# Feed-forward of three fused blocks: first pairs, sums of x, and the turn from up to down

## The chip, the core and the metric

The kernel runs on one core of one Trainium2 chip. The metric is the device time of one execution in microseconds (us), as the median of the runs shown. PE is the matmul engine (PEld its weight load), DVE the vector engine, ACT the scalar engine, POOL the GpSimd engine, and SP the engine that here only issues DMAs.

## What is computed

Three blocks run one behind another on x of 1024 tokens by 1024 features, all in float32. Blocks 1 and 2 end in a feed-forward of the same shape, and the change touches those two alone:

```
hn = norm(h)                                   # 1024 x 1024
g, up = jnp.split(hn @ w_ffn_in, 2, axis=-1)   # w_ffn_in 1024 x 5632
h = h + (jax.nn.silu(g) * up) @ w_ffn_out      # w_ffn_out 2816 x 1024
```

Block 1 has a root-mean-square norm ahead of it; block 2 has a layer norm and, between norm and feed-forward, a gated projection (the `ple` loop, L1207 to L1216). The up pass is the product with `w_ffn_in` and silu times up; the down pass is the product with `w_ffn_out` and the sum into h. "The turn" below is where one follows the other.

## The kernel before

**Two halves of every number.** A float32 operand x is kept as a high part `hi` (x rounded to fp32r) and a low part `lo` = x − hi. A product is three matmuls, hi·hi, hi·lo and lo·hi, added up in PSUM (`mm3`, L95 to L97); each is 128x128 by 128x512. So each operand that is loaded needs a cast (hi) and a subtraction (lo). For weights this is `weight` (L78 to L88): a DMA on SP's queue into one of two `w_raw` buffers, the cast on DVE (or on ACT where `hi_on` is set), the subtraction on POOL, into one of four pairs of buffers `w_hi`, `w_lo` of the pool `wp`.

**The up pass** (`ffn_up`) works on 22 pairs, each one column block of the gate weights and one of the up weights, with 128 features of the hidden layer. x lies in two halves of tokens, `x_fm[0]` (tokens 0 to 511) and `x_fm[1]` (512 to 1023).

- The first two pairs (`plain=2`) are plain products: 24 matmuls for each of g and u in each half of the tokens, 192 matmuls in all.
- The other 20 pairs use a scheme of seven products in place of eight (Strassen-Winograd), with x and the weights cut into quarters. A product is 12 matmuls, a pair 84. On the x side the products take, in their order, `b11`, `t1`, `t2`, `b21`, `t3`, `b12`, `b22`. The `b` are the quarters of x themselves, `t1` to `t3` sums of them, which `sums()` makes while the plain pairs run. `last_sums()` overwrites `b12`, which is a quarter of `x_fm[1]`, so it can only run when the plain pairs need `x_fm[1]` no more; its result is wanted by product 5 (counted from 0). Per k in 0 to 3 the sums are 4 subtractions or adds of 128x512 on POOL in `sums()` and 2 in `last_sums()`, and 5 and 2 on DVE.
- On the weight side `operands(fi)` makes seven operands for a pair: two loads of raw weights, four sums (one on POOL, three on DVE), seven casts on ACT, seven subtractions on POOL. An operand takes half of a `w_hi`, `w_lo` pair. These places come round in fives: four pairs in `wp`, and a fifth pair in the up pass's own pool. Six operands are made ahead (`more(AHEAD)`), then one behind each product (`more(1)`).
- The result of a pair, `ao`, is stored to `act_d` in HBM by SP, one half at a time.

**The down pass** takes the 22 row blocks of `w_ffn_out` in nine groups of two and a last group of four. `load` brings one block of activations back from `act_d` (SP's queue), ACT makes hi (L550), DVE makes lo (L551). A group is 16 sums of 128x512 in PSUM, each 12 matmuls for four blocks or 6 for two, and for each sum DVE adds into h (L562). The activations for the next group are asked for one group ahead. In block 1 the buffers for them come from twelve (`unit`, which held x and the sums), in block 2 from four (`unit_b`); each load takes whichever buffer comes free.

**The residual h** is written to HBM ahead of the up pass, since its place (32 KB of each partition) is used by the up pass: `t2` lies over h[4] to h[7], and the buffers `s` and the fifth pair `w_hi`, `w_lo` lie over h[0] to h[3]. It is read back at the turn by eight DMAs on ACT's queue (L570).

**Order.** The program's text sets priorities; a planner runs the text against a model of the engines and fixes each engine's order, so that a matmul that is ready in the model can pass one that is not. On the chip each engine then runs its list in order and waits by semaphores. SP's and ACT's DMA issues stand in such lists too.

Of the kernel before, what the change touches and what calls it, by code (L numbers as in the profile page):

```python
# [13 lines left out]
ALU = mybir.AluOpType  # L14
# [17 lines left out]
def kernel(ctx: ExitStack, tc: tile.TileContext, a, out, blocks=(1, 2, 3)):  # L32
# [15 lines left out]
    def f(ap):  # L48
        return ap.bitcast(F32)
# [80 lines left out]
    def fm(w, xh, nk=KD, k0=0, pt=None, start=True, stop=True):  # L130
        pt = mmtile() if pt is None else pt
        mm3(pt, [(kslice(w, k0 + k), xslice(xh, k, 0, HS)) for k in range(nk)], start, stop)
        return pt
# [243 lines left out]
    def ffn_up(pl, pp, unit, unit_r, x_fm, w_in, act_d, plain=2):  # L377

        half_k = lambda h, k: tuple(fm_.at[4 * k][0] for fm_ in x_fm[h])
        b11, b21, b12, b22 = half_k(0, 0), half_k(0, 1), half_k(1, 0), half_k(1, 1)
        t1, t3 = (tuple(four(unit(f"{n}{j}")) for j in range(2)) for n in ("t1", "t3"))
        t2 = tuple(four(unit_r(f"t2{j}")) for j in range(2))
        dve, pool_e = nc.vector.tensor_tensor, nc.gpsimd.tensor_tensor
        sl = [slice(0, HS), slice(HS, S)]
        tmp = lambda n: pl.tile([P, HS], F32, name=n, tag=n, bufs=2)

        def whole(n, x, k, eng):
            o = tmp(n)  # L390
            eng(out=o, in0=f(x[0][:, k]), in1=f(x[1][:, k]), op=ALU.add)
            return o

        def parts(x, k, src, eng):
            act(out=x[0][:, k], in_=src, func=AF.Copy)
            eng(out=x[1][:, k], in0=src, in1=f(x[0][:, k]), op=ALU.subtract)

        def sums():

            for k in range(4):  # L400
                x11, x12, x22 = whole("p1", b11, k, pool_e), whole("u2", b12, k, dve), whole("u3", b22, k, pool_e)
                dve(out=x11, in0=x12, in1=x11, op=ALU.subtract)
                parts(t1, k, x11, pool_e)
                yield
                dve(out=x12, in0=x22, in1=x12, op=ALU.subtract)
                parts(t3, k, x12, pool_e)
                dve(out=x22, in0=x22, in1=x11, op=ALU.subtract)
                parts(t2, k, x22, dve)
                yield

        def last_sums():

            for k in range(4):
                x21, y2 = whole("p1", b21, k, pool_e), whole("u2", t2, k, dve)
                dve(out=x21, in0=x21, in1=y2, op=ALU.subtract)
                parts(b12, k, x21, pool_e)

        def out_of(fi):
            ao = pl.tile([P, S], F32, name="ao", tag="ao", bufs=2)
            return ao, lambda h: nc.sync.dma_start(act_d[fi][:, sl[h]], ao[:, sl[h]])  # L420

        gen = sums()
        for fi in range(plain):
            wg, wu = weight(w_in[fi]), weight(w_in[F_TILES + fi])
            ao, store = out_of(fi)
            for h in (1, 0):
                g = fm(wg, x_fm[h])
                u = fm(wu, x_fm[h])
                silu_mul(pl, g, u, ao, sl[h])
                store(h)  # L430
                for _ in range(2 if fi < plain - 1 or h else 8):
                    next(gen, None)


        n_op, held = [0], []

        def slot():
            if n_op[0] % 2 == 0:
                i = n_op[0] // 2 % 5
                q, nb = (wp, 4) if i < 4 else (pl, 1)  # L440
                held[:] = [q.tile([P, 1024], F32R, name=n, tag=n, bufs=nb) for n in ("w_hi", "w_lo")]
            c = slice(n_op[0] % 2 * 512, n_op[0] % 2 * 512 + 512)
            n_op[0] += 1
            return tuple(x[:, c] for x in held)

        def operand(src, eng):
            hi, lo = slot()
            nc.scalar.copy(hi, src)  # L448
            eng(out=lo, in0=src, in1=f(hi), op=ALU.subtract)  # L449
            return hi, lo  # L450

        def operands(fi):
            raw = []
            for j in (F_TILES + fi, fi):
                r = wp.tile([P, 1024], F32, name="w_raw", tag="w_raw", bufs=2)
                nc.sync.dma_start(r, w_in[j])
                raw.append(r)
            (a21, a22), (a11, a12) = ((r[:, 0:512], r[:, 512:1024]) for r in raw)

            def mix(x, y, op, eng):  # L460
                s = pl.tile([P, 512], F32, name="s", tag="s", bufs=4)
                eng(out=s, in0=x, in1=y, op=op)
                return s
            yield operand(a11, pool_e)
            s1 = mix(a21, a22, ALU.add, pool_e)
            yield operand(s1, pool_e)
            s2 = mix(s1, a11, ALU.subtract, dve)
            yield operand(s2, pool_e)
            s4 = mix(a12, s2, ALU.subtract, dve)
            s3 = mix(a11, a21, ALU.subtract, dve)  # L470
            yield operand(a12, pool_e)
            yield operand(s3, pool_e)
            yield operand(a22, pool_e)
            yield operand(s4, pool_e)

        AHEAD = 6
        xs = (b11, t1, t2, b21, t3, b12, b22)
        ready = []

        def all_operands():  # L480
            for fi in range(plain, F_TILES):
                yield from operands(fi)
        source = all_operands()

        def more(n):
            for _ in range(n):
                w = next(source, None)
                if w is not None:
                    ready.append(w)
        more(AHEAD)  # L490
        last_sums()
        for fi in range(plain, F_TILES):
            ao, store = out_of(fi)

            def product(i, pt, start=True):
                w = ready.pop(0)
                mm3(pt, [(kslice(w, k), tuple(x[:, k] for x in xs[i])) for k in range(4)], start, onto=not start)
            pa, pd = mmtile("mm", 2), mmtile("mm", 2)
            pb, pc = (pp.tile([P, HS], F32, name=n, tag=n, bufs=1) for n in ("pb", "pc"))
            p1, u2, u3 = tmp("p1"), tmp("u2"), tmp("u3")  # L500
            product(0, pa)
            act(out=p1, in_=pa, func=AF.Copy)
            more(1)
            product(1, pc)
            more(1)
            product(2, pb)
            tt(out=u2, in0=p1, in1=pb, op=ALU.add)
            more(1)
            product(3, pa, False)
            sg = tmp("sg")  # L510
            act(out=sg, in_=pa, func=AF.Silu)
            more(1)
            product(4, pb, False)
            tt(out=u3, in0=p1, in1=pb, op=ALU.add)  # L514
            tt(out=p1, in0=u3, in1=pc, op=ALU.add)
            more(1)
            product(5, pd)
            tt(out=u3, in0=u3, in1=pd, op=ALU.add)
            tt(out=ao[:, sl[0]], in0=sg, in1=u3, op=ALU.mult)
            store(0)  # L520
            more(1)
            product(6, pc, False)
            tt(out=u2, in0=u2, in1=pc, op=ALU.add)
            act(out=u2, in_=u2, func=AF.Silu)
            tt(out=ao[:, sl[1]], in0=u2, in1=p1, op=ALU.mult)
            store(1)
            more(1)

    def ffn(x_fm, unit, unit_b, h, h_d, h_st, open_h, w_in, w_out, before_last, done, group=2):
# [9 lines left out]
        with ExitStack() as c:  # L539
            pool("down_edge", side="right", c=c).tile([P, 24], F32, name="edge")  # L540
            dp = pool("down", side="right", c=c)

            def load(fi, last):
                if last:
                    hi, lo = (dp.tile([P, S], F32R, name=f"act_{j}", tag=f"act_{j}", bufs=LAST) for j in ("hi", "lo"))
                else:
                    at = unit_b("act")
                    hi, lo = at[:, 0:S], at[:, S:2 * S]
                nc.sync.dma_start(f(lo), act_d[fi])
                act(out=hi, in_=f(lo), func=AF.Copy)  # L550
                nc.vector.tensor_tensor(out=lo, in0=f(lo), in1=f(hi), op=ALU.subtract)  # L551
                return hi, lo

            def down(fis, ats, done=None):
# [11 lines left out]
            groups = [list(range(g, g + group)) for g in range(0, F_TILES - LAST, group)]  # L566
            groups.append(list(range(F_TILES - LAST, F_TILES)))
            ats = [[load(fi, False) for fi in groups[0]]]
            for t in range(NT):
                nc.scalar.dma_start(h[t], h_d[t * P:(t + 1) * P])  # L570
            for i, fis in enumerate(groups[:-1]):
                nxt_g = groups[i + 1]
                ats.append([load(fi, nxt_g is groups[-1]) for fi in nxt_g])
                down(fis, ats[i])
            before_last()
            down(groups[-1], ats[-1], done)
            done.flush()
# [1056 lines left out]
```

## Time and profile before

| | |
|---|---|
| median of the 3 runs | 3503.18 us (3501.65 to 3503.7) |
| the profiled execution | 3509.02 us, its span 3507.3 us |
| mean granted clock of PE | 0.962 |
| feed-forward of block 1 in the span | about 716 to 1480 us, its turn at 1166 to 1201 us |
| feed-forward of block 2 in the span | about 2106 to 2820 us, its turn at 2546 to 2580 us |

The span runs from the first to the last instruction; the 1.7 us around it are start and end. The views give busy time by engine, the idle time ahead of an instruction and what ended it ("idle before", in brackets in a timeline), and the clock that PE was granted in a stretch.

### The profile page before, as it was taken

Reading aid. Unit: us, or ns where it says so; the run is one execution under the profiler, and the core shown is the slowest. Engines: PE = TensorE matmul, PEld = TensorE weight load, DVE = VectorE, ACT = ScalarE, POOL = GpSimd, SP = SyncE. Lnnn points to the kernel's source line nnn. Section 1 sums busy time; section 2 is a strip of 40 time slices with the busy share of each in tenths; the row PEclk is TensorE's granted clock in tenths of the full one; section 3 lists DMA queues with packets and bytes.
Section 4 is the critical chain, followed back from the end, with each engine's and each line's share of the span. In section 5 each row is a group of like instructions: output and inputs, shape, how many; then the busy total and the mean of one; then the engine's idle time right before and its main releaser. Section 6 shows DMA issues by size and latency. Waiting matters only on the chain. (4 is left out here: it accounts for less than half of the span.)

```text
span 3507.3 us, 40024 instructions
## 1 busy us (share of the span) xinstructions
PE 3278.3 (93%) x14976; PEld 2674.0 (76%) x14976; DVE 2169.9 (62%) x3300; ACT 1066.3 (30%) x2002; POOL 1368.6 (39%) x906
## 2 busy tenths in 40 slices
PE   8999999989999899999979998999989986889998
PEld 6888888877888678778768776888867865667776
DVE  5455456374444666557768847444467779985665
ACT  3333311132233200312145522323210133445552
POOL 3111131175555222134444348555412356552221
PEclk9999999999999999999989999999999998999899
DMA  4111124322222521222251132222342221122241
GB/s 138 65 62 62 55 66 132 127 66 78 82 83 83 216 73 58 75 88 94 87 180 49 37 108 75 81 81 88 105 148 96 85 75 38 49 91 73 77 144 66
DMA packets 111986, 310.12 MB, mean 88 GB/s; under 512 B 15744, under 2 KB 20992, under 8 KB 111792
## 3 DMA queue, kind: packets, MB, share of 16 engines
q1 hardware_dynamic: 79184, 240.75, 20.4%
q10 hardware_dynamic: 32560, 66.69, 5.6%
q8 instruction: 118, 1.93, 0.2%
q14 instruction: 76, 0.62, 0.1%
q0 software_dynamic: 48, 0.13, 0.0%
HBM read 235.62 MB, written 72.15 MB: 88 GB/s over the span
## 5 line engine op out<-in xcount | busy, mean ns | idle before, releaser
L87 POOL TENSOR_TENSOR w_lo<-w_raw,w_hi 128x1024 fp32r<-128x1024 f32 x187 | 467.1, 2499 | 1224.7 <-DVE w_hi L86 888.3
L95 PE MATMUL mm<-x,w_hi 128*128 128x512 f32 x688 | 278.4, 405 | 22.7 <-DVE kl L279 11.0
L96 PE MATMUL mm<-x,w_hi 128*128 128x512 f32 x688 | 277.7, 404 | 0.0
L97 PE MATMUL mm<-x,w_lo 128*128 128x512 f32 x688 | 274.9, 400 | 0.5 <-POOL w_lo L87 0.5
L86 DVE CAST w_hi<-w_raw 128x1024 fp32r<-128x1024 f32 x179 | 188.7, 1054 | 126.2 <-PE mm L96 57.3
L449 POOL TENSOR_TENSOR w_lo<-s,w_hi 128x512 fp32r<-128x512 f32 x160 | 220.4, 1385 | 113.6 <-ACT w_hi L448 112.1
L95 PE MATMUL mf<-x,w_hi 128*128 128x512 f32 x576 | 233.8, 406 | 16.4 <-DVE u L1299 14.2
L97 PE MATMUL mf<-x,w_lo 128*128 128x512 f32 x576 | 229.5, 398 | 1.2 <-POOL w_lo L87 1.2
L96 PE MATMUL mf<-x,w_hi 128*128 128x512 f32 x576 | 230.2, 400 | 0.0
L449 POOL TENSOR_TENSOR w_lo<-w_raw,w_hi 128x512 fp32r<-128x512 f32 x120 | 166.7, 1389 | 106.8 <-ACT w_hi L448 106.8
L562 DVE TENSOR_TENSOR h<-h,mm 128x512 f32<-128x512 f32 x214 | 145.0, 683 | 96.8 <-PE mm L97 88.6
L514 DVE TENSOR_TENSOR u<-p,pb 128x512 f32<-128x512 f32 x40 | 27.5, 687 | 267.1 <-PE pb L97 267.1
L95 PE MATMUL mm<-w_hi,act 128*128 128x512 f32 x384 | 153.6, 400 | 25.4 <-DVE h L562 24.9
L95 PEld LDWEIGHTS mm<-x,w_hi 128*128 128x128 f32 x688 | 132.2, 192 | 55.4 <-issue 24.0
L448 ACT CAST w_hi<-s 128x512 fp32r<-128x512 f32 x160 | 97.3, 619 | 236.5 <-PE pc L96 152.2
L1313 DVE SCALAR_TENSOR_TENSOR cy<-u,cols,cy 128x1024 f32<-128x1024 f32 x80 | 166.3, 2084 | 0.9
L97 PEld LDWEIGHTS mm<-x,w_lo 128*128 128x128 f32 x688 | 131.8, 192 | 28.9 <-issue 1.5
L96 PEld LDWEIGHTS mm<-x,w_hi 128*128 128x128 f32 x688 | 132.3, 192 | 27.0 <-issue 2.0
L96 PE MATMUL mm<-w_lo,act 128*128 128x512 f32 x384 | 151.4, 394 | 0.0
L97 PE MATMUL mm<-w_hi,act 128*128 128x512 f32 x384 | 151.2, 394 | 0.0
L335 ACT ACTIVATE st<-st,nmax 128x128 f32<-128x128 f32 (+5 forms) x192 | 119.3, 623 | 104.0 <-DVE nmax L329 99.5
L95 PEld LDWEIGHTS mf<-x,w_hi 128*128 128x128 f32 x576 | 110.9, 192 | 41.1 <-DVE u L1299 14.9
(506 smaller groups left out, 8971.0 us busy)
## 6 DMA issues: line engine op xcount, KB each, us to landing
w_raw<-in_w_ffn_in_dram SPq DMA_DIRECT2D x88, 512.0 KB, 3.7
w_raw<-in_w_in_dram SPq DMA_DIRECT2D x78, 512.0 KB, 3.5
act_d<-ao SPq DMA_DIRECT2D x88, 256.0 KB, 2.0
w_raw<-in_w_ffn_out_dram SPq DMA_DIRECT2D x44, 512.0 KB, 3.5
act<-act_d SPq DMA_DIRECT2D x36, 512.0 KB, 3.4
w_raw<-in_w_out_dram SPq DMA_DIRECT2D x24, 512.0 KB, 3.8
gates_d<-go SPq DMA_DIRECT2D x32, 256.0 KB, 2.0
gt<-gates_d ACTq DMA_DIRECT2D x32, 256.0 KB, 3.1
```

Of the source, the lines that this page charges most:

```text
L86: nc.vector.tensor_copy(hi, raw)
L87: nc.gpsimd.tensor_tensor(out=lo, in0=raw, in1=f(hi), op=ALU.subtract)
L95: mm(out_, lh, rh, start=start and i == 0, stop=False, **kw)
L96: mm(out_, lh, rl, start=False, stop=False, **kw)
L97: mm(out_, ll, rh, start=False, stop=stop and i == n - 1, **kw)
L335: act(out=st[:, :w + extra], in_=st[:, :w + extra], func=AF.Exp, scale=-1.0, bias=nmax, accum_out=ssum)
L448: nc.scalar.copy(hi, src)
L449: eng(out=lo, in0=src, in1=f(hi), op=ALU.subtract)
L514: tt(out=u3, in0=p1, in1=pb, op=ALU.add)
L562: tt(out=hh, in0=hh, in1=pt, op=ALU.add)
L1313: stt(out=y, in0=src, scalar=w, in1=y, op0=ALU.mult, op1=ALU.add)
```

## The change

It edits `ffn_up` and `ffn`, which both feed-forwards use.

- The first of the two plain pairs takes the halves of the tokens in the order 0, 1 instead of 1, 0; the second stays at 1, 0.
- `more(AHEAD)` stands ahead of the second plain pair instead of behind both.
- `last_sums()` becomes a generator; its four steps are taken one behind each of the first four products, where all four stood ahead of the first product.
- The pair of places for operands that lies in the up pass's own pool is used for the first of five instead of the last of five.
- All buffers of the up pass's pool are named at its start, which fixes their order in memory.
- Activations of the down pass go round in six fixed buffers, in both blocks (block 1: six of `unit`; block 2: four of `unit_b`, two of `unit`).
- The subtraction that makes an activation's lo moves from DVE to POOL (all 22 blocks of a down pass).
- The casts of `w_ffn_out` move from DVE to ACT for the nine groups ahead of the last one (`hi_on`).
- The eight loads of h move from ACT's queue to SP's.

```diff
+        for n, w, dt, nb in ([("ao", S, F32, 2)] + [(n, HS, F32, 2) for n in ("sg", "p1", "u2", "u3")] +
+                             [("s", HS, F32, 4), ("w_hi", 1024, F32R, 1), ("w_lo", 1024, F32R, 1)]):
+            pl.tile([P, w], dt, name=n, tag=n, bufs=nb)
...
                 parts(b12, k, x21, pool_e)
+                yield
...
-        gen = sums()
-        for fi in range(plain):
-            wg, wu = weight(w_in[fi]), weight(w_in[F_TILES + fi])
-            ao, store = out_of(fi)
-            for h in (1, 0):
-                g = fm(wg, x_fm[h])
-                u = fm(wu, x_fm[h])
-                silu_mul(pl, g, u, ao, sl[h])
-                store(h)
-                for _ in range(2 if fi < plain - 1 or h else 8):
-                    next(gen, None)
...
-                q, nb = (wp, 4) if i < 4 else (pl, 1)
+                q, nb = (wp, 4) if i else (pl, 1)
...
-        more(AHEAD)
-        last_sums()
+        gen = sums()
+        for fi in range(plain):
+            wg, wu = weight(w_in[fi]), weight(w_in[F_TILES + fi])
+            ao, store = out_of(fi)
+            last = fi == plain - 1
+            if last:
+                more(AHEAD)
+            for h in (1, 0) if last else (0, 1):
+                g = fm(wg, x_fm[h])
+                u = fm(wu, x_fm[h])
+                silu_mul(pl, g, u, ao, sl[h])
+                store(h)
+                for _ in range(2 if not last or h else 8):
+                    next(gen, None)
+
+        fours = last_sums()
...
                 mm3(pt, [(kslice(w, k), tuple(x[:, k] for x in xs[i])) for k in range(4)], start, onto=not start)
+                next(fours, None)
...
+            acts = []
+
             def load(fi, last):
...
-                    at = unit_b("act")
+                    if len(acts) < 6:
+                        acts.append((unit_b if len(acts) < 4 else unit)("act"))
+                    at = acts[fi % 6]
...
-                nc.vector.tensor_tensor(out=lo, in0=f(lo), in1=f(hi), op=ALU.subtract)
+                nc.gpsimd.tensor_tensor(out=lo, in0=f(lo), in1=f(hi), op=ALU.subtract)
...
             ats = [[load(fi, False) for fi in groups[0]]]
+            hi_on[0] = True
             for t in range(NT):
-                nc.scalar.dma_start(h[t], h_d[t * P:(t + 1) * P])
+                nc.sync.dma_start(h[t], h_d[t * P:(t + 1) * P])
...
+            hi_on[0] = False
             before_last()
```

## Rows read from the trace of the kernel before

**Rows 1.** The page: busy time of each engine, share of the span, instructions.

```profile
PE 3278.3 (93%) x14976; PEld 2674.0 (76%) x14976; DVE 2169.9 (62%) x3300; ACT 1066.3 (30%) x2002; POOL 1368.6 (39%) x906
```

**Rows 2.** Windows: length, busy time (instructions) by engine, granted clock, DMA share, GB/s.

```profile
715.60:812.20 96.60, 81.98 (x335) 65.49 (x334) 69.08 (x64) 29.32 (x51) 74.40 (x47) 0.89 0.20 62
900.00:1000.00 100.00, 100.00 (x443) 82.81 (x442) 45.64 (x54) 30.17 (x53) 54.69 (x42) 1.00 0.26 86
...
1165.80:1201.00 35.20, 20.30 (x65) 14.91 (x65) 25.98 (x26) 12.82 (x13) 4.21 (x2) 0.76 0.83 321
1220.00:1300.00 80.00, 78.58 (x341) 63.27 (x341) 54.76 (x69) 4.25 (x4) 14.42 (x6) 1.00 0.19 66
...
2139.80:2193.60 53.80, 42.36 (x158) 32.27 (x158) 37.45 (x34) 15.72 (x28) 45.03 (x31) 0.84 0.18 59
...
2546.00:2580.00 34.00, 23.80 (x86) 18.39 (x85) 18.43 (x23) 4.64 (x5) 5.07 (x2) 0.85 0.64 232
2600.00:2700.00 100.00, 97.31 (x420) 77.76 (x419) 72.38 (x86) 8.50 (x8) 19.24 (x8) 1.00 0.25 85
2700.00:2780.00 80.00, 78.65 (x342) 63.41 (x341) 55.33 (x68) 4.25 (x4) 19.21 (x8) 1.00 0.30 99
```

**Rows 3.** Timeline of PE at the first up pass's start: start, us, operation.

```profile
705.17 1.04 PE L158 MATMUL tr<-sq_c,xn 128*128 128x128 f32 x8
...
720.68 1.94 PE L158 MATMUL tr<-sq_c,xn 128*128 128x128 f32 x8 [2.74 <-DVE rstd L148]
...
733.33 0.63 PE L95 MATMUL mm<-h,w_hi 128*128 128x512 f32 x1
```

**Rows 4.** Windows of POOL alone, both starts: length, busy time (instructions), then as above.

```profile
726.10:781.40 55.30, 50.35 (x33) 0.90 0.10 34
2118.10:2181.10 63.00, 60.30 (x39) 0.87 0.16 50
```

**Rows 5.** Waits of PE at the second start: us in total, times, longest.

```profile
PE mm L96 <- POOL y L396: 7.0, 2, 4.1
```

**Rows 6.** Timeline of PE at both turns.

```profile
1154.96 0.39 PE L97 MATMUL pb<-t,w_lo 128*128 128x512 f32 x1
...
1172.43 0.79 PE L95 MATMUL pc<-h,w_hi 128*128 128x512 f32 x1 [3.48 <-DVE p L515]
...
1177.29 0.62 PE L97 MATMUL pc<-h,w_lo 128*128 128x512 f32 x1
...
1190.54 0.79 PE L95 MATMUL mm<-w_hi,act 128*128 128x512 f32 x1 [11.26 <-DVE h L562]
...
2560.16 0.79 PE L95 MATMUL mm<-w_hi,act 128*128 128x512 f32 x1 [5.14 <-DVE h L562]
...
2569.06 0.79 PE L95 MATMUL mm<-w_hi,act 128*128 128x512 f32 x1 [4.31 <-DVE h L562]
```

**Rows 7.** Timeline of ACT and its queue at the first turn.

```profile
1183.10 1.06 ACT L550 ACTIVATE act<-act 128x1024 fp32r<-128x1024 f32 x1 [0.61 <-DMA act<-act_d]
1183.12 9.22 ACTq L570 DMA_DIRECT2D h<-h_d  x8
```

**Rows 8.** Reads of activations, 1140 to 1201 us: issue ns min/median/max, first and last start.

```profile
L549 SPq DMA_DIRECT2D act<-act_d x12: 319/380/433, 1149.7 to 1177.9; - x12
```

**Rows 9.** Timeline of DVE at the first turn.

```profile
1168.72 3.06 DVE L551 TENSOR_TENSOR act<-act 128x1024 fp32r<-128x1024 f32 x1
```

**Rows 10.** A window at the first turn, columns as in Rows 2.

```profile
1183.00:1192.40 9.40, 1.86 (x4) 1.49 (x5) 3.25 (x4) 1.07 (x2) 0.00 (x0) 0.59 1.03 418
```

**Rows 11.** Groups of DVE, 2580 to 2780 us: count, busy us, mean ns, idle before.

```profile
L562 DVE TENSOR_TENSOR h<-h,mm 128x512 f32<-128x512 f32 x91 | 61.5, 683 | 39.2 <-PE mm L97 39.2
...
L86 DVE CAST w_hi<-w_raw 128x1024 fp32r<-128x1024 f32 x18 | 28.7, 1592 | 0.4
L551 DVE TENSOR_TENSOR act<-act 128x1024 fp32r<-128x1024 f32 x14 | 26.0, 1856 | 0.0
```

**Rows 12.** Groups of POOL, 2580 to 2780 us, columns as in Rows 11.

```profile
L87 POOL TENSOR_TENSOR w_lo<-w_raw,w_hi 128x1024 fp32r<-128x1024 f32 x18 | 43.3, 2403 | 180.3 <-DVE w_hi L86 174.2 <-PE mm L97 4.1 <-PE mf L97 1.4
```

## Prediction

> **What bounds the kernel now.** I read the page's busy times first: PE is busy 93% of the span and no other engine over 62% [rows 1], so PE's list of matmuls sets the end, and a change gains only where PE stands still or runs at its lower clock. Then windows over the two feed-forwards, to price that in one measure: in a stretch without waits PE ends 443 instructions in 100 us, 0.2257 us each [rows 2]; what a window is longer than its count times 0.2257 is lost, idle time and slow clock together. Five places lose, and the diff edits work at all of them.
>
> - Start 1 (715.6 to 812.2): 335 instructions, of them 32 transposes that take 1.04 us per eight where nothing holds them up [rows 3]. 303 × 0.2257 + 4.2 = 72.6 of 96.6: 24.0 lost.
> - Start 2 (2139.8 to 2193.6): 158 × 0.2257 = 35.7 of 53.8: 18.1 lost.
> - Turn 1: 65 × 0.2257 = 14.7 of 35.2: 20.5 lost. Turn 2: 86 × 0.2257 = 19.4 of 34.0: 14.6 lost.
> - Down passes, three windows: 341, 420 and 342 instructions in 80, 100 and 80 us: 3.0 + 5.2 + 2.8 = 11.0 lost [rows 2].
>
> Together 88 us, the most that the change can give. Next I read, in the timelines of PE and of what released it, what ends each wait.
>
> **Start 1: order of the halves.** PE ends the projection into h at 715.6 and then has only the transposes of the last token tiles, with waits between them, one of 2.74 us, on DVE, since each tile wants a norm first [rows 3]. The first matmuls of the up pass are in the second half of the tokens, which those transposes fill. The waits also cost clock: behind them a matmul stands at 0.63 us (733.33), the lower of the clock's two levels (1.2 and 2.4 GHz), where 0.39 is usual, and the granted clock over the whole start is 0.89 [rows 2, 3, 6]. With half 0 first, 48 matmuls (10.8 us) need nothing of those tiles; with the transposes' 4.2 they fill 715.6 to 730.6, just when the second half is whole. PE alone could then win all 24 us.
>
> POOL does not let it. It is busy 50.35 of the 55.3 us up to 781.4, when the last subtraction of `last_sums` is done, in 33 instructions, 1.53 us each [rows 4]. By count these are 16 for `sums`, 8 for `last_sums`, 2 adds and 6 subtractions for operands, and one weight. The sums need the second half of x, which no edit makes earlier. In the new text the last step of `last_sums` stands behind products 0 to 3 and so behind three more operands: 3 × 1.53 = 4.6 us, so product 5 can begin at 786.0. Of the 111 matmuls that PE has done by 812.2 behind the 192 plain ones, 60 belong to products 0 to 4; the plain ones end at 715.6 + 4.2 + 43.3 = 763.1, the 60 at 776.6, and PE waits 9.4 us. Behind 786.0 come the other 51, 11.5 us, and about 1.6 for the lower clock after the wait (eight matmuls with 0.2 more, an estimate from 0.63 against 0.39 in rows 3 and 6). That is 799.1 against 812.2: 13 us won. The bounds: 24 if POOL does its work in the gaps that it has; 8.5 if the planner lets three operands more pass (4.6 later).
>
> **Start 2.** Here a gated projection stands between norm and up pass, both halves of x are ready, and the order of halves gives nothing. PE waits for POOL: 7.0 us for the lo of `b12` (tile y, L396) [rows 5]. Up to that lo's end at 2181.1 POOL did 39 instructions, 1.55 us each and with 2.7 us idle [rows 4]; 12 of them were operands' subtractions, where the new text asks for 9 ahead of it. Three fewer are 4.6 us; I take 5. Bounds: 0 (the planner fills in as many as now) and the whole 18.
>
> The fifth place of operands moved to the front serves both starts: while the plain pairs hold all four places of `wp`, two operands can be made without them. It adds no work. What is added at the starts is nothing but order.
>
> **The turns.** Read turn 1 in order [rows 6]. PE stops for 3.48 us ahead of product 6, for DVE's L515; DVE was in a subtraction for an activation that took 3.06 us [rows 9]. On POOL such a subtraction holds up nothing that product 6 wants. Product 6 ends at 1177.3, and then PE stands for 11.26 us until DVE has added into h, which waits for h itself. The eight reads of h begin at 1183.12, at once behind a cast of an activation that ACT had been waiting for [rows 7]; they stand in ACT's list behind its casts, and since the fifth operand pair lies over h[2] and h[3] and is the last that products 5 and 6 read, two of them could not go ahead of product 6's end in any list. The DMA engines are full then: share 1.03 at 418 GB/s [rows 10]. Twelve activations have been asked for since 1149.7 [rows 8], and the last group's four come beside h: 16 of 512 KB, 8.4 MB, or 20 us at that rate, ahead of or beside h's 4.2 MB (10 us).
>
> After the change the last thing that h waits for is `t2`, whose last matmul starts at 1154.96 [rows 6]; `s` and the fifth pair are free before. Eight issues on SP and 10 us of transfer then end near 1166, and with six buffers only six activations can be in front. PE would begin product 6 near 1169 (1172.43 less its wait) and want h[0] 2.7 us later. What is new on the way is POOL's: two activations and two weights for the first group, 4 × 2.40 = 9.6 us [rows 12], half of the 19 us from the first activation's request to 1169. ACT gets the weights' casts, about as long as an activation's 1.06 us [rows 7]; with these they are four, 4.2 us, in a group of 16 × 6 × 0.2257 = 21.7 us. I leave 5 us at each turn for ends that don't meet: 20.5 − 5 = 15.5 and 14.6 − 5 = 9.6, where the waits are 5.14 and 4.31 [rows 6]. Bounds: all of it, or 8 and 3 (below).
>
> SP's queue gets the eight issues in front of group 1's two activations and two weights, 2.1 MB. All that groups 0 and 1 need, with h, is 8.4 MB, 20 us at 418 GB/s; even begun at 1149.7 it is done by 1170, well ahead of group 1's start near 1172 + 21.7 = 1193. So that move costs nothing while group 0 covers it; without that cover it is h's 10 us.
>
> **The down passes.** In 2580 to 2780 us DVE spends 28.7 us on casts of weights and 26.0 on activations' subtractions, in pieces of 1.6 and 1.86 us, between adds of 0.68 that free PSUM [rows 11]. Both go. POOL, which now does 18 weights there in 43.3 us [rows 12], gets 14 activations more, 33.6 us in 200: room enough. Of the 11.0 lost I take 6; bounds 0 and 11.
>
> There is a rule against it. The Trainium skill, SBUF — State Buffer, section "SBUF: two separate sides", says that DVE and GpSimd share one port pair as an exclusive lock, which a DVE instruction with two SBUF inputs also takes while GpSimd reads SBUF. If the add into h took part, 22 subtractions of 2.4 us would block it in each down pass, and the down passes would win nothing, so that the sum would be 43; but one of its inputs is in PSUM. The trace agrees: its mean is 683 ns with POOL busy 43.3 of the 200 us [rows 11, 12].
>
> **Sum.** 13 + 5 + 15.5 + 9.6 + 6 = 49 us. The profiled execution took 3509.0 (span 3507.3 and 1.7 around it) and would come to 3460; the median is 5.8 lower, so 3454.
>
> **Rivals.**
>
> - *POOL keeps both starts.* If the planner fills POOL with operands ahead of `last_sums`, PE only waits later and longer. For it: POOL is busy 91 and 96% there [rows 4]. Against it: at start 1 PE's waits stand ahead of half 1 and not behind POOL [rows 3]. Starts 0, the rest 31: 3472.
> - *h behind the activations in one queue.* On ACT's queue h shared the engines with SP's transfers; on SP's it goes behind whatever SP has issued or waits on. If SP stands on a store of `ao` (its last come with the end of the up pass) or on six activations (3.1 MB, 7.5 us), h lands that much later: turns give 8 and 3 instead of 25, and the total is 35: 3468. The Trainium skill, DMA: Bandwidth & Descriptors, section "Queues, rings and completion order", speaks for it: an engine takes turns between queue rows packet by packet, so that a row of its own is an advantage for h. No run shows yet which weighs more here.
> - *Both of these:* 17 won, 3486.
> - *Slower: h is late by more than now.* One mechanism, h in SP's list behind transfers that need the end of the up pass. Each 512 KB ahead of it is 1.25 us at 418 GB/s. To eat the 24 us of starts and down passes and 7 more (0.2%), h would have to land 31 + 25 us late over both turns beyond my forecast, some 22 transfers at each turn; the last group's four and all the rest of six buffers are ten. At 22 it decides; 3510 then. Planner orders are not seen in the text, so it keeps a chance.
>
> **Numbers.** My forecast 0.57, POOL's rival 0.2, h's 0.11, both 0.06, slower 0.06. 0.2% (7 us) is about what a measurement here tells from no change; I count 0.02 of "both" and 0.01 of the slower rival as within it, so 0.92 faster, 0.03 same, 0.05 slower. The range runs from half-way to the good bounds (start 1 +6, start 2 +5, turns +8, down +3: 71 won, 3432) to "both" at 3486; outside it lie the slower rival, half of "both" and some 0.08 at the fast end.
>
> **What the profile would show.** Right: matmuls of tile h between the transposes after 716; reads of h issued before the up pass ends and no wait of PE on DVE L562 above 2 us at the turns; L551's successor on POOL at about 2.4 us; POOL still without gaps at the starts and PE's longest wait there for the lo of `b12`. Wrong, if PE's waits at the turns stay above 5 us or POOL's last lo of `b12` comes later than now.

## Result and profile after

The changed kernel took 3470.66 us (median of 4 runs, 3464.67 to 3475.9) against 3503.44 before: a ratio of 0.9907 with a 95% interval of 0.9888 to 0.9926, 32.8 us or 0.9% faster. The forecast was 3454 with a range of 3432 to 3486. The profiled span went from 3507.3 to 3472.1 us.

To see where it came from, I cut each span at ends of the same DVE instructions: the second half of the 18th pair in each up pass (start 1, start 2), the 15th addition to h behind it (turn), the 135th or 157th (down pass), and the first product of silu and up (L375) of the second up pass (between). Each column is the time since the one before it. The kernels below the first two are the experiments.

| kernel | start 1 | turn 1 | down 1 | between | start 2 | turn 2 | down 2 | rest | median |
|---|---|---|---|---|---|---|---|---|---|
| before | 1137.8 | 72.9 | 167.1 | 746.1 | 394.8 | 67.2 | 228.0 | 693.4 | 3503.44 |
| after | 1125.9 | 66.1 | 163.2 | 746.6 | 389.8 | 66.1 | 219.0 | 695.5 | 3470.66 |
| e_early | 1126.9 | 51.0 | 163.2 | 747.2 | 384.3 | 52.2 | 219.0 | 689.3 | 3435.0 |
| e_actq | 1125.5 | 62.6 | 163.2 | 740.2 | 391.0 | 62.9 | 219.0 | 686.7 | 3456.33 |
| e_dvecast | 1127.5 | 65.2 | 164.2 | 746.4 | 390.1 | 66.4 | 220.2 | 686.6 | 3472.08 |
| e_start | 1125.2 | 76.4 | 167.1 | 738.9 | 389.8 | 69.2 | 228.0 | 686.4 | 3488.79 |
| e_lo_dve | 1125.7 | 64.3 | 167.9 | 744.4 | 389.8 | 65.8 | 223.7 | 690.4 | 3473.78 |
| e_four | 1125.0 | 68.1 | 163.2 | 743.8 | 390.0 | 68.9 | 219.0 | 688.7 | 3468.58 |
| e_halves | 1126.5 | 65.4 | 163.2 | 743.1 | 389.8 | 66.0 | 219.0 | 688.9 | 3463.71 |
| e_nospread | 1135.9 | 66.5 | 163.2 | 744.4 | 399.5 | 65.4 | 219.0 | 692.8 | 3488.48 |
| e_spread | 1131.9 | 67.8 | 163.2 | 744.2 | 392.6 | 66.2 | 219.0 | 688.8 | 3475.45 |
| e_ahead | 1125.5 | 65.8 | 163.2 | 747.3 | 389.8 | 65.6 | 219.0 | 690.2 | 3468.04 |
| e_early_spread | 1133.5 | 62.2 | 163.2 | 752.9 | 386.9 | 62.3 | 219.0 | 688.7 | 3467.11 |
| e_early_halves | 1132.2 | 51.0 | 163.2 | 752.3 | 384.4 | 52.2 | 219.0 | 691.9 | 3445.77 |

Medians are of 4 to 6 runs, but of a single run for e_lo_dve, e_four, e_halves, e_nospread, e_spread and e_ahead; stages are from one profiled execution each. The ratios given for experiments are to runs of the kernel before that were made beside them (medians 3500.98, 3507.09 and 3500.54). In the three e_early kernels L375 ends 15 us behind the first silu's end in place of 10, so 5 us of their start 2 stand under "between". How far one program's stages differ by themselves is seen in e_ahead: by the trace's names every engine and every DMA queue runs the same list there as in the changed kernel, and starts, turns and down passes agree within 0.5 us, "between" within 0.7, but "rest" is 5.3 apart. So 11.9 us came at start 1, 5.0 at start 2, 6.8 and 1.1 at the turns, 3.9 and 9.0 in the down passes; 0.5 and 2.1 were lost in stretches that the change does not touch. That makes up the 35.2 us of the span, up to rounding; the 2.1 in "rest" are less than e_ahead's 5.3.

Busy times of the changed kernel (page; compare [rows 1]): DVE does 100 us less, POOL 108 more, and PE's share rises by a point.

```profile
PE 3255.7 (94%) x14976; PEld 2662.9 (77%) x14976; DVE 2069.9 (60%) x3220; ACT 1101.3 (32%) x2038; POOL 1476.1 (43%) x950
```

Windows of the changed kernel, columns as in [rows 2]: start 1, start 2, the 20 us around each turn's wait, and the second down pass.

```profile
714.50:799.80 85.30, 75.33 (x332) 59.78 (x330) 68.78 (x62) 27.75 (x48) 73.92 (x45) 0.98 0.21 67
...
1162.70:1182.70 20.00, 10.04 (x36) 8.10 (x37) 7.03 (x9) 1.58 (x2) 9.36 (x4) 0.74 0.88 333
...
2107.50:2165.40 57.90, 48.23 (x198) 37.46 (x196) 46.09 (x37) 15.80 (x29) 53.19 (x34) 0.97 0.16 50
...
2528.50:2548.50 20.00, 9.74 (x37) 7.83 (x37) 7.00 (x9) 1.58 (x2) 9.49 (x4) 0.74 0.90 323
...
2570.00:2670.00 100.00, 100.00 (x443) 82.84 (x442) 50.38 (x74) 18.56 (x19) 41.20 (x18) 1.00 0.30 93
2670.00:2750.00 80.00, 80.00 (x354) 65.99 (x353) 47.49 (x69) 6.55 (x6) 24.32 (x13) 1.00 0.23 75
```

The down pass now runs at the steady rate (443 in 100 us, as in [rows 2]): nothing is left to win there. At each turn 20 us hold 36 or 37 instructions, 8.1 to 8.4 us of work by 0.2257 us each; about 12 us are lost, some 10 in the wait and the rest to the clock, granted at 0.74. Timeline of PE at the two turns, to be read beside [rows 6]. The first line is the last matmul that reads `t2` (product 2 of the last pair); on DVE the sum that closes product 2, L514, follows at 1143.47:

```profile
1142.97 0.39 PE L97 MATMUL pb<-t,w_lo 128*128 128x512 f32 x1
...
1172.66 0.79 PE L95 MATMUL mm<-w_hi,act 128*128 128x512 f32 x1 [9.97 <-DVE h L573]
...
2538.87 0.79 PE L95 MATMUL mm<-w_hi,act 128*128 128x512 f32 x1 [10.26 <-DVE h L573]
```

The wait ahead of product 6 (3.48 us at turn 1) is gone, but one long wait for h stands at each turn, at turn 2 longer than the two longest of before together (5.14 + 4.31). What is late can be followed back through three timelines of turn 1. ACT:

```profile
1164.34 1.04 ACT L84 CAST w_hi<-w_raw 128x1024 fp32r<-128x1024 f32 x1 [4.29 <-DMA w_raw<-in_w_ffn_out_dram]
1165.29 0.62 ACT L531 ACTIVATE u<-u 128x512 f32<-128x512 f32 x1
```

DVE:

```profile
1159.29 0.69 DVE L530 TENSOR_TENSOR u<-u,pc 128x512 f32<-128x512 f32 x1 [1.49 <-PE pc L97]
1165.95 1.61 DVE L532 TENSOR_TENSOR ao<-u,p 128x512 f32<-128x512 f32 x1 [5.98 <-ACT u L531]
1171.92 0.69 DVE L573 TENSOR_TENSOR h<-h,mm 128x512 f32<-128x512 f32 x1 [4.36 <-DMA h<-h_d]
```

SP's queue:

```profile
1160.08 0.33 SPq L80 DMA_DIRECT2D w_raw<-in_w_ffn_out_dram  x1
1160.50 0.38 SPq L424 DMA_DIRECT2D act_d<-ao  x1
1164.74 0.33 SPq L80 DMA_DIRECT2D w_raw<-in_w_ffn_out_dram  x1
1167.59 0.32 SPq L424 DMA_DIRECT2D act_d<-ao  x1
1167.96 3.90 SPq L582 DMA_DIRECT2D h<-h_d  x8
```

The last silu (L531) has its input at 1160.0 (end of L530), but stands behind a weight's cast on ACT that waits for the weight's read. So the product L532 and its store come at 1165.95 and 1167.59, and the reads of h stand behind that store in SP's list. They are issued at 1167.96, some 25 us behind the last matmul that reads `t2`; the first addition follows 4 us later. The transfers were not the limit until then: in the 5 us before, the DMA engines moved 198 GB/s, against 365 in the 10 us behind (windows of the changed kernel):

```profile
1163.00:1168.00 5.00, 0.00 (x0) 0.00 (x0) 1.61 (x1) 1.58 (x2) 5.00 (x3) 0.84 0.57 198
1168.00:1178.00 10.00, 5.34 (x15) 4.24 (x16) 3.08 (x5) 0.00 (x0) 4.06 (x2) 0.57 0.96 365
```

### The profile page after: what moved, and what is told of

Its sections match the earlier page's. It is cut to its first block, busy times and chain, and to the rows that moved or that the text cites. A ratio compares the mean times of both kernels' runs of the same rounds, so it can differ in the third digit from the quotient of the medians.

```text
span 3472.1 us, 39991 instructions
## 1 busy us (share of the span) xinstructions
PE 3255.7 (94%) x14976; PEld 2662.9 (77%) x14976; DVE 2069.9 (60%) x3220; ACT 1101.3 (32%) x2038; POOL 1476.1 (43%) x950
## 5 line engine op out<-in xcount | busy, mean ns | idle before, releaser
L86 DVE CAST w_hi<-w_raw 128x1024 fp32r<-128x1024 f32 x143 | 133.7, 936 | 125.2 <-PE mm L96 56.1
L440 ACT CAST w_hi<-s 128x512 fp32r<-128x512 f32 x160 | 96.9, 619 | 222.2 <-PE pc L96 148.5
```

What stands on the lines that cost most here:

```text
L86: nc.vector.tensor_copy(hi, raw)
```

## Experiments at the turn

**e_early: h ahead of the last stores.** In the changed kernel the reads of h stand behind the up pass's last store, where the pool closes that lay over h. Here what the last store needs lies elsewhere, and the pool over h (t2, s, one weight pair) can close first.

```diff
-    def ffn_up(pl, pp, unit, unit_r, x_fm, w_in, act_d, plain=2):
+    def ffn_up(pl, pr, pp, unit, unit_r, x_fm, w_in, act_d, plain=2):
...
-            pl.tile([P, w], dt, name=n, tag=n, bufs=nb)
+            (pr if n in ("s", "w_hi", "w_lo") else pl).tile([P, w], dt, name=n, tag=n, bufs=nb)
...
+        lc = ExitStack()
+        upl = pool("up_l", c=lc)
...
             for t in range(NT):
                 nc.sync.dma_start(h[t], h_d[t * P:(t + 1) * P])
+            lc.close()
+            dp = pool("down", side="right", c=c)
```

> The changed kernel with the tiles ao, sg, p1, u2 and u3 of the up pass moved to the other side of SBUF, so that the eight h tiles lie only over t2, s and one weight pair; SP then lists the reads of h ahead of the last two stores of the up pass, and two of the activation reads behind them. Nothing is left out. Theory A (PE's wait of 9.97 and 10.26 us at the turns is set by when SP issues h, which is behind the last store): both waits fall to 3 us or less, the first addition to h at each turn comes 7 to 10 us sooner, and the profiled span is 14 to 20 us under the changed kernel's 3472.1. Theory B (the transfers themselves set it: h and the activations are 18 reads through one set of queues, and whatever is read first the other lands late): PE waits about as long as now, on an activation cast in place of the addition to h, and the span is within 4 us of 3472.1.

It took 3435.0 us (3434.24 to 3440.7), 0.9817 of before (0.9802 to 0.9832), and its span is 39.0 us under the changed kernel's. PE has no wait at all at either turn. SP's queue at turn 1, and the one wait of a read of h in it (the fourth, from 1140.0 to 1143.17, until the last matmul that reads `t2` has ended):

```profile
1136.90 0.33 SPq L424 DMA_DIRECT2D act_d<-ao  x1
1137.62 0.82 SPq L560 DMA_DIRECT2D act<-act_d  x2
1138.50 5.46 SPq L582 DMA_DIRECT2D h<-h_d  x5
1147.91 0.32 SPq L424 DMA_DIRECT2D act_d<-ao  x1
1148.28 1.40 SPq L582 DMA_DIRECT2D h<-h_d  x3
1149.78 1.04 SPq L560 DMA_DIRECT2D act<-act_d  x2
1150.91 0.56 SPq L80 DMA_DIRECT2D w_raw<-in_w_ffn_out_dram  x1
1151.56 1.29 SPq L560 DMA_DIRECT2D act<-act_d  x2
...
SPq L582 <- PE pb L97: 3.1, 1, 3.1
```

And the 40 us around the turn, as windows:

```profile
1141.40:1161.40 20.00, 20.00 (x90) 16.57 (x89) 8.96 (x11) 7.43 (x9) 12.33 (x5) 1.00 1.00 378
1161.40:1181.40 20.00, 20.00 (x90) 16.57 (x89) 10.52 (x17) 10.50 (x11) 19.48 (x10) 1.00 0.68 244
```

The reads come 29 us sooner, the same transfers fill the DMA engines (378 GB/s) while the last pair still runs, and PE ends 90 instructions in 20 us straight through. Theory A holds, and its gain was set too low: the turns take 15.1 and 13.9 us less, since with the wait the slow clock behind it goes too. The other 10.0 of the 39.0 us lie in "between" and start 2 (4.9) and "rest" (6.2), less 1.0 at start 1; nothing here shows that they belong to the edit. Against before they are 21.9 and 15.0 us shorter; the prediction had priced the losses there at 20.5 and 14.6. Theory B is out: activations behind h were not late.

**e_actq: h on ACT's queue.**

```diff
-                nc.sync.dma_start(h[t], h_d[t * P:(t + 1) * P])
+                nc.scalar.dma_start(h[t], h_d[t * P:(t + 1) * P])
```

> The changed kernel with the reads of h issued by ScalarE's queue again, all else as changed. They stand there right behind the last silu, and so need neither the last product on VectorE nor the last store. Theory A1 (the silu is late because it stands behind a weight cast that waits for its read, and the step from silu to h through VectorE, the store and SP's queue is only 2.7 us of the wait): h is issued about 2 us sooner, PE's waits at the turns fall from 10 to about 8 us, the span by about 4. Theory A2 (as my rival of the one queue had it: the store and the single queue are what holds h back): the waits fall to 5 us or less, and the span by 10 or more.

3456.33 us, 0.9877 (0.9862 to 0.9891). ACT and its queue at turn 1:

```profile
1162.98 1.04 ACT L84 CAST w_hi<-w_raw 128x1024 fp32r<-128x1024 f32 x1 [4.37 <-DMA w_raw<-in_w_ffn_out_dram]
1163.03 0.96 ACTq L582 DMA_DIRECT2D h<-h_d  x2
1163.93 0.62 ACT L531 ACTIVATE u<-u 128x512 f32<-128x512 f32 x1
1164.03 12.01 ACTq L582 DMA_DIRECT2D h<-h_d  x6
```

The waits fell to 6.7 and, at turn 2, 8.2 us, the turns by 3.5 and 3.2. That is between the two theories and nearer to A1: the way from the silu over the store to SP's issue is worth about 3 us, and most of the wait lies ahead of it, where h still stands behind ACT's cast and the read that it waits for. The planner put two of the reads ahead of the silu; of the six behind it, five were issued only from 1171.92 on, later than in the changed kernel. Of the 14 us in the median only 6.7 came from the turns; the rest is in "between" and "rest", of which below.

**e_dvecast: no weight cast ahead of the last silu.**

```diff
-            hi_on[0] = True
```

> The changed kernel with the casts of the down projection's weights on VectorE as before the change, all else as changed; reads of h still on SP. The last silu then has no weight cast ahead of it on ScalarE. Theory A1: the last silu ends 4 to 5 us sooner at each turn, h is issued as much sooner, and PE's waits at the turns fall from 10 to 5 or 6 us. In the down passes the 18 casts of 1.59 us each are back on VectorE: 0 to 6 us given back there, so the span is 4 to 10 us lower. Theory A2: the waits stay near 10 us, and the span is equal or higher.

3472.08 us, 0.9918 (0.9903 to 0.9933): no gain. The silu did come sooner, as A1 has it (ACT; this kernel's up pass stands 1.6 us later, so 4.2 us in all):

```profile
1162.71 0.63 ACT L531 ACTIVATE u<-u 128x512 f32<-128x512 f32 x1 [1.53 <-DVE u L530]
```

But in SP's queue two weight reads and a store now stand directly ahead of h:

```profile
1162.46 2.16 SPq L80 DMA_DIRECT2D w_raw<-in_w_ffn_out_dram  x2
1164.84 0.33 SPq L424 DMA_DIRECT2D act_d<-ao  x1
1165.26 5.42 SPq L581 DMA_DIRECT2D h<-h_d  x8
```

From the issue to the first addition (1171.68) it took 6.4 us in place of 4.0, and PE waited 8.9 and 8.3 us. So A1 was half right: the cast makes the silu late, but taking it away only brings h to the next thing in the queue. The cure is the place in the list, not the chain that fills it. The casts on DVE cost the down passes 1.0 and 1.2 us.

**e_four: four buffers for activations.**

```diff
-                    if len(acts) < 6:
-                        acts.append((unit_b if len(acts) < 4 else unit)("act"))
-                    at = acts[fi % 6]
+                    if len(acts) < 4:
+                        acts.append(unit_b("act"))
+                    at = acts[fi % 4]
```

> The changed kernel with four buffers for the activations in turn in place of six, so that a group's reads wait for the group two before it; all else as changed. By the same two stretches. Theory C: they stay within 1 us of 163.2 and 219.0, the turns too. Theory D: they go back to 166 us or more and 226 us or more.

Down passes to the tenth as after. The waits at the turns rose to 12.6 and 13.1 us, the turns to 68.1 and 68.9: the two further buffers are worth 2.0 and 2.8 us there and nothing in the down passes. Theory C holds for these, but not its "turns too".

**e_lo_dve: activations' low parts on DVE.**

```diff
-                nc.gpsimd.tensor_tensor(out=lo, in0=f(lo), in1=f(hi), op=ALU.subtract)
+                nc.vector.tensor_tensor(out=lo, in0=f(lo), in1=f(hi), op=ALU.subtract)
```

> The changed kernel with the subtraction of the activations' low parts on VectorE again, all else as changed. Read by stage: the first down pass from the 15th to the 135th of its 160 additions to h took 167.1 us before and 163.2 after the change, the second from the 15th to the 157th 228.0 and 219.0. Theory C (the subtractions of 1.86 us, in VectorE's list ahead of additions to h that free PSUM, were what the down passes lost): they go back to about 166 to 167 and 226 to 228 us. Theory D (the six buffers, which let activations be read two groups ahead, gave it): they stay within 1 us of 163.2 and 219.0.

167.9 and 223.7 us: 4.7 us worse in each pass. Theory C holds in full for the first and for half of the second's 9.0; with the casts (1.0 and 1.2) this gives 5.9. The remaining 3 may come when both stand in DVE's list together, which was not tried by itself with the changed turn; in the first pass the two losses come to 5.7, more than the 3.9 gained, so they do not simply add. On POOL the subtractions and the additions to h did not disturb each other (groups of the changed kernel, 2545 to 2745 us; compare [rows 11, 12]):

```profile
L573 DVE TENSOR_TENSOR h<-h,mm 128x512 f32<-128x512 f32 x96 | 66.0, 688 | 64.5 <-PE mm L97 64.5
...
L562 POOL TENSOR_TENSOR act<-act 128x1024 fp32r<-128x1024 f32 x12 | 28.6, 2404 | 0.0
```

## Experiments at the starts

**e_start: the start's edits on the kernel before.** The loads, casts, subtractions and reads of the turn and the down passes are those of before.

> The kernel before with the part of the change that lies in the up pass alone: order of the halves, the first six operands ahead of the last plain tile, the sums of b12 spread over the products, the tiles' places. Loads, casts, subtractions and reads of h at the turns and in the down passes are as before. If the parts add, as the shifts between the two traces say (10.7 us at the first start, 4 at the second), the span is 13 to 16 us under 3507.3 and the time about 3489; PE's losses at the turns stay at 20.5 and 14.6 us, those in the down passes at 11. If the shifts mislead, and the early gain is eaten by the turns (an earlier up pass meets the same late activations), the span is within 5 us of 3507.

3488.79 us, 0.9972 (0.996 to 0.9985). The starts keep their whole gain (12.6 and 5.0 us), but the old turns give 3.5 and 2.0 of it back. That is not because h came as late as before: at turn 1 its reads are issued at 1170.66 for 1183.12, as much sooner as the up pass. But PE now waits twice for additions to h, 8.35 and 5.09 us, and before the second wait ends, DVE stands 7.31 us at the last group's subtraction (L560) for ACT's cast. Why the orders came out so was not tried, and only one execution was profiled.

**e_halves and e_nospread: one edit of the start undone each.**

```diff
-            for h in (1, 0) if last else (0, 1):
+            for h in (1, 0):
```

```diff
         fours = last_sums()
+        for _ in fours:
+            pass
```

The expectations call their point "the second store of the first pair"; the 835.6 and 819.8 us are the second half of the second pair.

> The changed kernel with the second half first in both plain tiles, as before the change; the operands ahead of the last plain tile, the spread sums and the rest as changed. Read at the first start, from the kernel's begin to the second store of the first pair: 835.6 us before, 819.8 after. Theory E (the order of the halves, which puts products of the finished half between the last transposes, gave most of the first start): 6 to 10 us later than after the change. Theory F (the spread of the sums of b12 over the products gave most): within 3 us of it.

> The changed kernel with the four sums of b12 listed all at once ahead of the first pair, as before the change, the rest as changed. Same stretch, up to the second store of the first pair. Theory E: within 3 us of the changed kernel's 819.8 us. Theory F: 6 us later or more.

At that point e_halves stood at 823.9 and e_nospread at 833.7; at the 18th pair, where the starts' effects have settled, they are 0.6 and 10.0 us later than the changed kernel. At the point named e_halves is 4.1 us later than the changed kernel, between the two theories, and e_nospread 13.9, as F has it; by the 18th pair E has fallen and F holds. The order of the halves brings the first product of silu and up 17.5 us forward (753.6 to 736.1), and almost all of it is lost again before the 18th pair, where 0.6 us is about what e_ahead differs by itself. At start 2 the spread is worth 9.7 us and the halves nothing. Waits of PE in e_nospread, 690 to 850 us, the two longest:

```profile
PE mm L95 <- ACT w_hi L440: 8.2, 1, 8.2
PE mm L96 <- POOL h L399: 2.6, 1, 2.6
```

That cast of a weight operand (L440) stands in ACT's list behind two casts of the sums (L398), each of which waits for its sum on DVE:

```profile
776.80 0.63 ACT L398 ACTIVATE h<-p 128x512 fp32r<-128x512 f32 x1 [7.73 <-DVE p L418]
780.14 0.63 ACT L398 ACTIVATE h<-p 128x512 fp32r<-128x512 f32 x1 [2.71 <-DVE p L418]
780.68 1.12 ACT L440 CAST w_hi<-s 128x512 fp32r<-128x512 f32 x2
```

In the changed kernel operands pass between the sums, and its waits in that stretch are 3.0 us at most.

**e_spread and e_ahead: which edits the spread needs.** e_ahead lists the six operands behind both plain tiles, as before; e_spread does so too and has the old halves and the old turn of operand places.

```diff
-            if last:
-                more(AHEAD)
...
+        more(AHEAD)
         fours = last_sums()
```

> The changed kernel with all of the start's edits but one as before: second half first in both plain tiles, the six operands behind both of them, the places of operands in the old turn; the sums of b12 stay spread over the first four products. Turns and down passes as changed. Read at the end of the 18th pair's second half in the first up pass (before 1137.8, after 1125.9, with the sums listed at once 1135.9) and from the second up pass's first silu to the same point there (before 394.8, after 389.8, sums listed at once 399.6). Theory G (the spread alone carries the starts, and what goes with it costs 5 us at the second): 1129 or less, and 387 or less. Theory H (the spread gains only because the operands ahead are ready by then): 1132 or more, and 391 or more.

> The changed kernel with the first six operands listed behind both plain tiles, as before, the rest as changed. Same two stretches. Theory G: within 2 us of 1125.9, and 387 or less. Theory H: 1130 or more, and 391 or more.

e_ahead is equal to the changed kernel (1125.5 and 389.8), and both theories had expected a difference at start 2. The reason is plain from the trace: the planner made the same lists of it on every engine, so this edit does nothing, and the run is the changed kernel once more. e_spread gains 5.9 and 2.2 us where the whole gains 11.9 and 5.0. So the spread carries about half alone, and the rest comes only together with the other edits; as halves undone alone cost 0.6 and the operands' place in the text changed no list, the turn of the places is what is left, or it together with another. That was not tried by itself, and stays open.

**e_early_spread and e_early_halves: the same on the fastest kernel.**

> The kernel with h ahead of the last stores, which took 3435.0 us, and of the start's edits only the spread of the sums. By theory G it gains the 5 us of the second start and loses 1 to 3 at the first: 3430 to 3434. By theory H it loses 5 to 10: 3440 to 3445. Turns stay without a wait of PE above 1 us in both.

> The kernel with h ahead of the last stores, with the second half first in both plain tiles as before the change. If the order of the halves is worth as little here as in the changed kernel (0.6 us), the time is within 3 us of 3435.0; if it gains only now that PE's list is shorter, it is 5 us or more above.

3467.11 us (0.9906, 0.9889 to 0.9923) and 3445.77 (0.9842, 0.9822 to 0.9861): both slower than e_early. e_early_spread lost 6.6 and 2.6 us at the starts, as H says, and, as neither theory had it, 11.2 and 10.1 at the turns, where PE waits again (its waits of PE, 1130 to 1240 us):

```profile
PE mm L95 <- DVE h L572: 6.9, 1, 6.9
```

With the old turn of places the last pair's products 5 and 6 read the weight pair that lies over h, so h cannot be read before they end. Product 6 ends at 1167.32, and h is issued at 1169.62, behind a weight's read and a store that SP's list has in between; e_early, with the new turn, issued it at 1138.5. So the line of the change that moves that pair to the first place of five is the likely cause of the 10 us a turn, once h is asked for early; in the changed kernel, where h comes late anyway, it was worth 1.7 and 0.1 (e_spread's turns). The halves are not the cause, since e_early_halves kept both turns at 51.0 and 52.2; the operands listed sooner, which made no difference in e_ahead, were not tried apart from it here, so the cause is argued and not isolated. e_early_halves lost 5.3 us at start 1, so on this kernel the order of the halves counts; the other half of its 10.8 us lies in "between" and "rest".

## Why the prediction came out as it did

The time lay in the range, 17 us above the forecast. By number it is nearest to "POOL keeps both starts" (3472), which the stages rule out, and next to "h behind the activations in one queue" (3468), whose mechanism is the one the traces show. That the sum came so near is in part luck: the turns gave 17.2 us less than forecast, the down passes 6.9 more, and the starts came out right for a wrong reason. Of the forecast's terms:

- **Start 1, 13: right in size (11.9), wrong in reason.** By the measure of [rows 2], 332 instructions in 85.3 us lose 10.4, where 335 in 96.6 lost 21.0. Matmuls of h do stand between the transposes. But product 5 does not wait for the whole of `b12`, as my 786.0 had it: it begins at 781.94 with the first quarter, and other products run between its four steps. And I took the order of the halves as the source and the spread as a delay of 4.6 us. It was the reverse: the spread is worth 10.0, the halves 0.6. My own sign of an error was there: POOL's last low part of `b12` ends at 799.7, later than the 781.4 of [rows 4], and PE loses little by it (0.84 us in its wait for it), since the products around it can run. Lines of PE and POOL in the changed kernel:

```profile
781.94 0.39 PE L95 MATMUL mm<-h,w_hi 128*128 128x512 f32 x1
...
798.40 1.27 POOL L399 TENSOR_TENSOR h<-p,h 128x512 fp32r<-128x512 f32 x1 [3.22 <-ACT h L398]
```

- **Start 2, 5: right in size (5.0), by two terms of opposite sign.** With the start's other edits but without the spread it is 4.7 us slower than before (399.5 against 394.8); the spread gives 9.7.
- **The turns, 15.5 and 9.6: the step that failed** (6.8 and 1.1). I wrote that the last thing h waits for is `t2`, that eight issues on SP and 10 us of transfer then end near 1166, and left 5 us. That is when h's place in SBUF is free, not when SP comes to the issue. The place was free even sooner (`t2` was last read at 1142.97), but SP's list had h behind the last store; the first h was asked for at 1167.96. My sign of being wrong, waits of PE above 5 us at the turns, was there too: 9.97 and 10.26. I had this as a rival at 0.11, with 11 of the turns' 25 us left; 7.9 came. e_early, where h is asked for at 1138.5, shows that the losses were there to be had in full, and that full DMA engines, which I read off [rows 10], were not the bound: in e_early they are as full (share 1.00 at 378 GB/s), but while the last pair still runs.
- **The down passes, 6: too small** (12.9). In the windows shown PE runs at its full rate, so all of the loss went there, and I had priced only 260 us of the two passes. I named the lock rule of the Trainium skill, SBUF — State Buffer, section "SBUF: two separate sides", and argued that the additions to h have one input in PSUM and escape it; their 688 ns beside POOL's subtractions agree.
- **POOL keeps both starts:** out, 16.9 us came. **Slower:** out; h was 10 us late at each turn, eight transfers' time by the rival's 1.25 us, and not 22.
- **A row of its own for h.** The Trainium skill, DMA: Bandwidth & Descriptors, section "Queues, rings and completion order", lets engines take turns between queue rows. e_actq gained 3 us a turn with it, but it also issued the first three reads of h 5 us sooner (1163.03 to 1164.03 for 1167.96 to 1168.92), so the runs don't show a gain of the row as such. e_early on SP's row needed none.

## What to carry to other kernels

When a transfer's destination is free, ask next where its issue stands in the list of the engine that issues it, and what every entry ahead of it waits for; here a store behind a silu behind a weight cast held back for some 25 us eight reads whose place was free at 1143.4. Buffers that must live until the last store should not share a pool with those that the next stage's loads overwrite, and the loop of rotating places should be turned so that the overlapping one is not used last (the runs here make the second likely and do not isolate it). An edit of a planned program's text can leave every planned list as it was, as e_ahead's did. A wait on PE costs more than its length by the slow clock behind it, so the gain of removing it is to be read from a window (36 instructions for 90), not from the wait alone; and totals of versions should be compared stage by stage.

## What was unexpected in the hardware

**The clock differs where the program doesn't.** The changed kernel and e_ahead run the same instructions in the same order on every engine, and in "rest" took 695.5 and 690.2 us. Most of the difference arises in 20 us of an attention stage with short waits. Windows of the changed kernel:

```profile
3346.00:3356.00 10.00, 9.42 (x35) 6.96 (x34) 7.50 (x24) 6.30 (x18) 0.00 (x0) 0.58 1.04 401
3356.00:3366.00 10.00, 9.42 (x37) 6.73 (x35) 7.56 (x23) 6.06 (x16) 0.00 (x0) 0.74 0.10 35
```

The same stretch in e_ahead:

```profile
3345.50:3355.50 10.00, 8.30 (x42) 5.73 (x43) 9.53 (x29) 8.81 (x24) 0.00 (x0) 1.00 1.03 391
3355.50:3365.50 10.00, 10.00 (x53) 7.66 (x51) 9.30 (x26) 5.67 (x15) 0.00 (x0) 1.00 0.16 60
```

72 instructions against 95, with the clock at 0.58 and 0.74 against 1.00. Over all kernels "between" spans 738.9 to 752.9 us and "rest" 686.4 to 695.5, though no edit lies there (5 us of the spread in "between" come from the place of the cut in the e_early kernels); in some kernels the planner's order differs there too, so the runs don't part the two causes. It may be why the changed kernel's runs lie 11 us apart; only one of them was profiled, so that is not shown.

**DVE stands still while POOL subtracts, if both its inputs are in SBUF.** The product L526 has both (sg and u). In the changed kernel's timeline it runs into a subtraction on POOL that ends at 1157.26:

```profile
1155.67 2.13 DVE L526 TENSOR_TENSOR ao<-sg,u 128x512 f32<-128x512 f32 x1
...
1154.85 2.41 POOL L562 TENSOR_TENSOR act<-act 128x1024 fp32r<-128x1024 f32 x1 [3.43 <-ACT act L561]
```

In e_early, with POOL idle from 1153.8 to 1159.0:

```profile
1155.44 0.69 DVE L526 TENSOR_TENSOR ao<-sg,u 128x512 f32<-128x512 f32 x1
```

2.13 against 0.69 us, and it ends 0.5 us behind POOL's subtraction, a little less than its own length. The last pair's L532 (1165.95, above), with both inputs in SBUF too, took 1.61 us beside POOL's next subtractions, which adds 0.9 us to the chain ahead of h. This fits the lock that the Trainium skill, SBUF — State Buffer, section "SBUF: two separate sides", names, seen in an instruction where I had not looked for it.
